# Conditioning products placed in four 32-column groups of the array, their parts summed by the product that transposes them

## The chip, the core and the metric

The kernel runs on one core of one Trainium2 chip. The metric is device time in microseconds (us); of several runs the median is taken. The core has a tensor engine (PE, with its weight loads shown apart as PEld), a vector engine (DVE), a scalar engine (ACT), GpSimd (POOL), and SyncE (SP), whose queue issues all the DMAs of this kernel.

## The reference, cut to what matters

The program computes a two-layer backbone over 1024 latent and 256 context tokens with 1024 channels. Each layer is steered by a conditioning vector; the change lies in how these conditioning values are computed, all in float32:

```
sc, scc = silu(c), silu(c_ctx)                                # 1024 each
for i in range(2):
    shift, scale, gate = split(sc @ ada_w[i] + ada_b[i], 3)         # ada_w[i]: 1024 x 3072
    shift_c, scale_c, gate_c = split(scc @ ada_w[i] + ada_b[i], 3)
    n_l = rmsnorm(h, norm_w[i]) * (1 + scale) + shift
    n_c = rmsnorm(hc, norm_w[i]) * (1 + scale_c) + shift_c
    y_l, y_c = layer_i(n_l, n_c)
    h, hc = h + gate * y_l, hc + gate_c * y_c
```

Layer 0 is retention and RWKV-7 side by side, layer 1 a Hyena convolution and neighbourhood attention.

## The kernel before, in words

The work comes in phases. `phase_a` (0 to some 690 us) norms the tokens, turns them channel-major and modulates them (`mod_tile`), projects them, and runs retention. `phase_b` (some 690 to 1290 us) runs RWKV in ten groups of 128 tokens, each with two recurrence steps (`recur`) and an inverse by 31 substitutions on DVE (lines 950 and 952). The later phases (output projection, second layer) follow.

The two conditioning vectors are kept as two columns, `self.sc`, [128, 8, 2]: channel k x 128 + p is in row p of slice k. `ada_block` (line 315) loads a block of n columns of `ada_w` as [128, 8, n] into a tile `aw`, and multiplies: eight products, the two columns of slice k stationary, the n columns of the weights moving, all added up in rows 0 and 1 of one PSUM tile `adaps` (line 321). A float32 product is shown in the trace as two matmul records with a weight load each, called passes here: 16 passes per block.

What is done with the two rows of sums differs:

- `ada_quarter` (layer 0, n = 256, eight blocks in the first 58 us): DVE copies the rows to SBUF (`adarow`, line 304), PE transposes each 128 columns by a product with a 2 x 2 identity (`adat`, line 307), DVE adds the bias. `mod_tile` needs the result.
- `ada_cols` (layer 1's shift and scale, n = 128, 16 blocks): the same with lines 284, 287 and 289.
- `ada_gate` (the gates of both layers, n = 128, 16 blocks): DVE adds the bias rows `adab` (two small DMAs, line 334, into a tile with one buffer) to the sums (line 335), and a DMA writes them to DRAM (line 336). Nothing is transposed.

In `phase_b` the 32 blocks of 128 columns are side work: first the gate of layer 0 (8 blocks), then `ada_cols` (16), then the gate of layer 1 (8). They share a PSUM pool with one buffer (`b_hp`, tag `mm`) with `RwkvOut`, which finishes RWKV's blocks. RWKV has a higher priority, and the planner that lays out each engine's instructions by simulated times fills the side work into the gaps. On the chip every engine then takes its instructions in that fixed order: an instruction that waits holds back all behind it on its engine.

Products that write only a part of PSUM's 128 rows use only the columns of the array that belong to these rows. `recur` has such products, 64 columns wide: at line 990 and 996 their outputs alternate between rows 0 to 63 and 64 to 127, at line 1002 eight go to one half, then eight to the other.

Of the kernel before, what the change touches and what calls it, by code (L numbers as in the profile page):

```python
# [10 lines left out]
F32 = mybir.dt.float32  # L11
# [3 lines left out]
ALU = mybir.AluOpType  # L15
AX = mybir.AxisListType
# [20 lines left out]
# ---------------------------------------------------------------- host layout  # L37
# [51 lines left out]
def dft_constants():  # L89
    """Two-stage DFT of 2048 real points, n = 8 n1 + n2, k = k1 + 256 k2, k1 = 0..127 with k1 = 128 in the place of the  # L90
    imaginary part of k1 = 0."""
# [69 lines left out]
def na_bias_layout(rpb):  # L161
    """[8, 15, 31] -> [8 heads, 2 row blocks, 3 column classes, 128 queries, 384 keys], with a fill outside the window."""
# [47 lines left out]
# ---------------------------------------------------------------- the kernel  # L210


class K:
# [23 lines left out]
    def ln_exp(self, out, x, scale, bias=None):  # L237
        """out = (scale x + bias) ** -0.5."""
        nc = self.nc
        if bias is None:  # L240
            nc.scalar.activation(out, x, AF.Ln, scale=scale)
        else:
            nc.scalar.activation(out, x, AF.Ln, scale=scale, bias=bias)
        nc.scalar.activation(out, out, AF.Exp, scale=-0.5)

    def rsqrt(self, pool, x, tag, n=1):
        """x: [P, n] positive -> its reciprocal square root; x is overwritten."""
# [16 lines left out]
    # ---- conditioning: 2 x 3072 modulation values per layer  # L264
    def ada_prepare(self, pool):
# [6 lines left out]
        self.sc = sc  # L272

    def ada_cols(self, layer, n, pool, psp, wbufs):
        """The column tile [P, (shift 8 | scale' 8), 2] of a layer's modulation, n columns at a time; a generator."""
# [5 lines left out]
        for blk in range(2048 // n):  # L281
            ps = self.ada_block(layer, blk * n, n, pool, psp, wbufs)
            rows = pool.tile([2, n], F32, name="adarow", tag="adarow", bufs=2)
            nc.vector.tensor_copy(rows, ps)
            pt = psp.tile([P, m, 2], F32, name="adat", tag="mm")
            for j in range(m):
                nc.tensor.matmul(pt[:, j, :], rows[:, j * P:(j + 1) * P], self.ident[0:2, 0:2], start=True, stop=True)
# [8 lines left out]
    def ada_quarter(self, layer, q, pool, psp, wbufs):  # L296
        """[P, (shift 2 | scale' 2), 2] of channel tiles 2 q, 2 q + 1."""
# [3 lines left out]
        for j in range(2):  # L301
            ps = self.ada_block(layer, j * DM + q * 256, 256, pool, psp, wbufs)
            rows = pool.tile([2, 256], F32, name="adarow", tag="adarow", bufs=2)
            nc.vector.tensor_copy(rows, ps)
            pt = psp.tile([P, 2, 2], F32, name="adat", tag="mm")
            for k in range(2):
                nc.tensor.matmul(pt[:, k, :], rows[:, k * P:(k + 1) * P], self.ident[0:2, 0:2], start=True, stop=True)
# [7 lines left out]
    def ada_block(self, layer, c0, n, pool, psp, wbufs):  # L315
# [4 lines left out]
        for k in range(8):  # L320
            nc.tensor.matmul(ps[0:2, :n], self.sc[:, k, :], w[:, k, :], start=k == 0, stop=k == 7)  # L321
        return ps[0:2, :n]

    def ada_gate(self, layer, n, pool, psp, wbufs):
        """A DRAM tile with the gate rows [2, 1024]; a generator."""
        nc = self.nc
        gd = self.gate[layer] = self.dram(f"gate{layer}", [2, DM])
        for c0 in range(0, DM, n):
            ps = self.ada_block(layer, 2048 + c0, n, pool, psp, wbufs)
            rows = pool.tile([2, n], F32, name="adarow", tag="adarow", bufs=2)  # L330
# [4 lines left out]
            nc.vector.tensor_tensor(rows, ps, ab, op=ALU.add)  # L335
            nc.sync.dma_start(gd[:, c0:c0 + n], rows)
            yield

    def norm_tile(self, xt, pool, tag):
        """xt [P, DM] token-major -> xt * rstd, in a tile of its own."""  # L340
# [9 lines left out]
    def modT(self, xns, t0, nhi, nlo, mc, v, pool, psp):  # L350
        """Normed token tiles xns (up to 4) -> columns t0.. of the transposed, modulated activations, split."""
# [3 lines left out]
    def mod_tile(self, xns, t0, nhi, nlo, k, sc, sh, pool, psp):  # L355
        """Channel tile k of it."""
# [11 lines left out]
    def wsplit(self, src, c0s, n, pool, tag="w", bufs=2, lo_eng=None, praw=None):  # L368
        """n columns of src [(8 P), .], in equal parts from each of c0s -> hi, lo float32r tiles [P, 8, n]."""
# [13 lines left out]
    def wtiles(self, src, c0s, pool, bufs, n=512):  # L383
        """512 columns of src, in equal parts from each of c0s -> hi(k), lo(k): float32r [P, 512], each in a tile of its
        own."""
# [15 lines left out]
    def mm3(self, ps, lh, ll, rh, rl, nk=8, start=True, stop=True):  # L401
        """ps += l.T @ r in three float32r passes; lh(k) etc. give operands."""
# [3 lines left out]
    def mm3_parts(self, ps, lh, ll, rh, rl, nk=8, start=True, stop=True):  # L406
        """mm3, as a generator that stops after every k."""
# [9 lines left out]
# ---------------------------------------------------------------- layer 0: projections and retention  # L417


def phase_a(s, D):  # L420
    """Activations, their projections, and retention. D: dict of DRAM tiles for what later phases read."""
# [56 lines left out]
class Shift:  # L478
    """RWKV's channels, channel-major, mixed with their neighbours in time."""
# [35 lines left out]
    def tokens(self, S, p):  # L515
        """S token-major, and with the tokens of each block of 128 in reverse."""
# [14 lines left out]
    def normed(self, S, p):  # L531
        """S of the k channels over the norm of its head's."""
# [13 lines left out]
    def run(self):  # L546
# [18 lines left out]
        # decay and rate activations  # L565
# [8 lines left out]
class Dense:  # L574
    """Retention's q, k, v (token-major, rotated) and the two gates, 512 columns of the projection at a time."""
# [18 lines left out]
    def qk(self, g):  # L594
        """Pairs 2g, 2g + 1: [pair][token][(q q k k v v), 64]."""
# [37 lines left out]
    def gate(self, nm, c0, turned):  # L633
        """2 silu(z), channel-major if turned."""
# [26 lines left out]
class Retention:  # L661
# [26 lines left out]
    def pair(self, p):  # L688
        """Heads 2p, 2p+1."""
# [89 lines left out]
# ---------------------------------------------------------------- layer 0: RWKV-7  # L779


def nat_block(d, g):
    """The 128-token block that direction d handles in group g: the context's two first, then the latent tokens'."""
# [3 lines left out]
def eye_lanes():  # L787
    """Row s = 2 i + l of the identity of 32, for lanes l * 64 + u: [P, 16, 32]."""
# [7 lines left out]
class Rwkv:  # L796
    """RWKV-7 in chunks of 64 tokens; groups of 2 chunk steps x 8 heads x 2 directions = 32 units. A unit index within a
    direction is (head parity h, step t, head pair p)."""
# [3 lines left out]
    def __init__(self, s, D, pg, pl, pc, pi, pf, pb):  # L802
# [14 lines left out]
        # operands that fill the tensor engine's rows, with zeros in the other head's, direction's or block's place  # L817
# [1105 lines left out]
```

## Time and profile before

| | |
|---|---|
| median of 3 runs | 2481.54 us (2480.74 to 2485.9) |
| span of the profiled execution | 2478.6 us |
| PE busy | 2301.3 us (93%), 16928 matmul passes |
| DVE busy | 1195.7 us (48%) |
| ACT, POOL busy | 931.3 us (38%), 786.5 us (32%) |
| passes of the conditioning products | 640, busy 111.8 us |
| mean granted TensorE clock | 0.941 |

The span goes from the first to the last instruction of one profiled execution; the median of the runs is 2.9 us longer. Busy time counts a pass from its start to its modelled end, so passes that overlap are counted once, and a busy PE is not PE at its peak. The granted clock is the share of full speed that the tensor engine had in a stretch.

### The profile page before, as it was taken

What the parts mean: (1) busy time and instruction counts of PE and PEld (TensorE: products, weight loads), DVE (VectorE), ACT (ScalarE), POOL (GpSimd) and SP (SyncE); (2) the same over time, 40 slices, a digit from 0 to 9 for tenths busy, and PEclk for the clock granted to TensorE, in tenths of its full rate; (3) what the DMA queues carried; (4) which work ended last, traced back from release to release, by engine and by line L of the source; (5) the groups of instructions that cost most, each with busy time, mean ns of one, the idle gap of its engine ahead of it and who ended that gap; (6) DMA issues with size and microseconds to landing.
All of it is one profiled execution on the core that took longest, in us unless ns stands there. A gap on an engine that the chain in (4) does not pass through costs nothing. (4 is left out here: it accounts for less than half of the span.)

```text
span 2478.6 us, 44427 instructions
## 1 busy us (share of the span) xinstructions
PE 2301.3 (93%) x16928; PEld 1879.3 (76%) x16928; DVE 1195.7 (48%) x3043; ACT 931.3 (38%) x1996; POOL 786.5 (32%) x1036
## 2 busy tenths in 40 slices
PE   7999999999988888888798999999899999989997
PEld 3778878777756777777686889889767777778987
DVE  6301212233348787677876546410145555534438
ACT  4321133545364444344254433321134333334432
POOL 2313617443656333333134433421101000010133
PEclk9999999999998677788898999999999999999999
DMA  7323334534386335565354334342465252265463
GB/s 241 94 72 111 109 113 139 162 113 127 107 227 177 84 99 135 135 146 142 82 169 147 125 120 137 121 150 76 118 176 149 84 143 71 63 202 150 127 187 124
DMA packets 398302, 325.68 MB, mean 131 GB/s; under 512 B 134974, under 2 KB 337864, under 8 KB 397834
## 3 DMA queue, kind: packets, MB, share of 16 engines
q1 hardware_dynamic: 398090, 322.85, 45.1%
q8 instruction: 134, 2.20, 0.4%
q14 instruction: 78, 0.64, 0.1%
HBM read 227.58 MB, written 95.17 MB: 130 GB/s over the span
## 5 line engine op out<-in xcount | busy, mean ns | idle before, releaser
L380 POOL TENSOR_TENSOR wlo<-wraw,whi 128x512 fp32r<-128x512 f32 (+1 forms) x60 | 81.7, 1379 | 414.6 <-ACT whi L379 351.7
L412 PE MATMUL dps<-n1hi,whi 128*128 128x512 f32 x448 | 195.1, 436 | 0.0
L412 PE MATMUL dps<-n1hi,wlo 128*128 128x512 f32 x448 | 177.0, 395 | 0.0
L412 PE MATMUL dps<-n1lo,whi 128*128 128x512 f32 x448 | 176.7, 394 | 0.0
L412 PE MATMUL dnp<-wlo,nhi 128*128 128x512 f32 x400 | 159.5, 400 | 2.9 <-POOL wlo L396 2.9
L412 PE MATMUL dnp<-whi,nlo 128*128 128x512 f32 x400 | 158.5, 398 | 0.0
L412 PE MATMUL dnp<-whi,nhi 128*128 128x512 f32 x400 | 154.7, 402 | 1.3 <-ACT whi L395 1.3
L396 POOL TENSOR_TENSOR wlo<-wraw,whi 128x512 fp32r<-128x512 f32 (+1 forms) x72 | 92.1, 1288 | 133.4 <-ACT whi L395 133.1
L412 PE MATMUL mmps<-nhi,whi 128*128 128x512 f32 (+1 forms) x336 | 123.4, 368 | 3.3 <-ACT vto L527 2.1
L321 PE MATMUL adaps<-aw,sc 128*2 128x128 f32 (+1 forms) x640 | 111.8, 330 | 11.7 <-DMA aw<-in_ada_w 10.0
L412 PE MATMUL mmps<-nlo,whi 128*128 128x512 f32 (+1 forms) x336 | 120.7, 361 | 0.0
L412 PE MATMUL mmps<-nhi,wlo 128*128 128x512 f32 (+1 forms) x336 | 119.4, 364 | 0.0
L950 DVE TENSOR_TENSOR tm<-RR,AL 128x126 f32<-128x126 f32 (+22 forms) x310 | 101.0, 326 | 18.8 <-DMA AL<-la 12.6
L412 PEld LDWEIGHTS dps<-n1hi,whi 128*128 128x128 f32 x448 | 84.8, 189 | 32.5 <-issue 21.7
L1248 POOL TENSOR_TENSOR hn<-hn,xr 128x256 f32<-128x256 f32 x60 | 47.2, 791 | 171.3 <-DVE hn L1247 159.3
L952 DVE TENSOR_TENSOR RR<-RR,tm 128x126 f32<-128x126 f32 (+22 forms) x310 | 96.8, 312 | 6.2
L412 PEld LDWEIGHTS dps<-n1hi,wlo 128*128 128x128 f32 x448 | 84.8, 189 | 18.8
L321 PEld LDWEIGHTS adaps<-aw,sc 128*2 128x2 f32 x640 | 54.7, 93 | 55.1 <-issue 15.2
L412 PE MATMUL ops<-whi,clo 128*128 128x256 f32 x320 | 90.6, 291 | 5.4 <-DVE clo L1181 5.4
L412 PEld LDWEIGHTS dps<-n1lo,whi 128*128 128x128 f32 x448 | 85.3, 190 | 10.5
L412 PEld LDWEIGHTS dnp<-wlo,nhi 128*128 128x128 f32 x400 | 76.0, 190 | 22.3 <-POOL wlo L396 4.6
L412 PE MATMUL ops<-wlo,chi 128*128 128x256 f32 x320 | 91.7, 288 | 0.0
(399 smaller groups left out, 6245.3 us busy)
## 6 DMA issues: line engine op xcount, KB each, us to landing
aw<-in_ada_w SPq DMA_DIRECT2D x32, 512.0 KB
kkr<-kkr SPq DMA_DIRECT2D x40, 384.0 KB
wraw<-in_odd_w_in SPq DMA_DIRECT2D x56, 256.0 KB
wraw<-in_even_w_in SPq DMA_DIRECT2D x48, 256.0 KB
bi<-in_nab SPq DMA_DIRECT2D x64, 192.0 KB
aw<-in_ada_w SPq DMA_DIRECT2D x8, 1024.0 KB
spec<-KS SPq DMA_DIRECT2D x32, 256.0 KB
h<-hn SPq DMA_DIRECT2D x16, 512.0 KB
```

Of the source, the lines that this page charges most:

```text
L321: nc.tensor.matmul(ps[0:2, :n], self.sc[:, k, :], w[:, k, :], start=k == 0, stop=k == 7)
L380: (lo_eng or nc.gpsimd).tensor_tensor(lo[:, kk:kk + 4], raw, hi[:, kk:kk + 4].bitcast(F32), op=ALU.subtract)
L396: nc.gpsimd.tensor_tensor(lo[:, :n], raw[:, :n], hi[:, :n].bitcast(F32), op=ALU.subtract)
L412: nc.tensor.matmul(ps, a, b, start=start and n == 0, stop=stop and n == 3 * nk - 1)
L950: nc.vector.tensor_tensor(t3, RR[:, 0:n, q:q + 1].to_broadcast([P, n, w]), AL[:, q:q + 1, q + 1:32].to_broadcast([P, n, w]), op=ALU.mult)
L952: nc.vector.tensor_tensor(RR[:, 0:n, q + 1:32], RR[:, 0:n, q + 1:32], t3, op=ALU.add)
L1248: add.tensor_tensor(h[:, cs], h[:, cs], x[:, cs], op=ALU.add)
```

## The change

Only the conditioning is changed, and the descriptor space of GpSimd's own DMAs. The stationary operand becomes 32 columns wide (two with values, 30 with zeros). Product k writes rows 32 (k mod 4) to 32 (k mod 4) + 31 of PSUM, so each of the four row groups holds the sum of two of the eight slices. The whole [128, n] PSUM tile is copied to SBUF, and the transposing product uses, in the place of the 2 x 2 identity, a matrix `sel` [128, 2] that has ones at the rows 32 g + j of column j: it adds the four parts as it transposes. For the gates, which were not transposed, a product with `sel` as the stationary operand is new (`adag`); its sums get the bias in the `adab` tile, from which they are written out.

```
 def ada_prepare
-        self.sc = sc
+        self.sc = self.cp.tile([P, 8, 32], F32, name="scw")
+        nc.gpsimd.memset(self.sc, 0.0)
+        nc.vector.tensor_copy(self.sc[:, :, 0:2], sc)
+        self.sel = self.cp.tile([P, 2], F32, name="sel")
+        nc.vector.tensor_reduce(self.sel, self.ident.rearrange("p (g c) -> p c g", g=4)[:, 0:2, :], axis=AX.X, op=ALU.add)
 def ada_cols (and ada_quarter, with 256 for n)
-            rows = pool.tile([2, n], F32, name="adarow", tag="adarow", bufs=2)
+            rows = pool.tile([P, n], F32, name="adarow", tag="adarow", bufs=2)
             nc.vector.tensor_copy(rows, ps)
...
-                nc.tensor.matmul(pt[:, j, :], rows[:, j * P:(j + 1) * P], self.ident[0:2, 0:2], start=True, stop=True)
+                nc.tensor.matmul(pt[:, j, :], rows[:, j * P:(j + 1) * P], self.sel, start=True, stop=True)
 def ada_block
         for k in range(8):
-            nc.tensor.matmul(ps[0:2, :n], self.sc[:, k, :], w[:, k, :], start=k == 0, stop=k == 7)
-        return ps[0:2, :n]
+            g = 32 * (k % 4)
+            nc.tensor.matmul(ps[g:g + 32, :n], self.sc[:, k, :], w[:, k, :], start=k < 4, stop=k > 3)
+        return ps[:, :n]
 def ada_gate
-            rows = pool.tile([2, n], F32, name="adarow", tag="adarow", bufs=2)
+            rows = pool.tile([P, n], F32, name="adarow", tag="adarow", bufs=2)
...
-            nc.vector.tensor_tensor(rows, ps, ab, op=ALU.add)
-            nc.sync.dma_start(gd[:, c0:c0 + n], rows)
+            nc.vector.tensor_copy(rows, ps)
+            ps = psp.tile([P, 512], F32, name="adag", tag="mm")
+            nc.tensor.matmul(ps[0:2, :n], self.sel, rows, start=True, stop=True)
+            nc.vector.tensor_tensor(ab, ps[0:2, :n], ab, op=ALU.add)
+            nc.sync.dma_start(gd[:, c0:c0 + n], ab)
 def kernel
-    nc = bacc.Bacc("TRN2", target_bir_lowering=False, num_devices=1)
+    nc = bacc.Bacc("TRN2", target_bir_lowering=False, num_devices=1, dynamic_dma_scratch_size=4096)
```

The new columns take 1 KB more of each SBUF partition; the last line gives GpSimd's own DMA descriptors less of it.

## Rows read from the trace of the kernel before

**Rows 1.** The stretches of the program: busy us of each engine with its instructions, the granted clock (PEclk), the DMA engines' busy share and GB/s. Columns: from:to, length, PE, PEld, DVE, ACT, POOL, PEclk, DMA, GB/s.

```profile
62.00:640.00 578.00, 560.38 (x2812) 439.83 (x2811) 146.60 (x288) 204.98 (x366) 241.57 (x344) 0.99 0.39 115
690.00:747.00 57.00, 51.86 (x399) 36.80 (x398) 33.77 (x78) 38.02 (x98) 34.64 (x53) 0.97 0.81 219
747.00:800.00 53.00, 47.83 (x311) 35.58 (x312) 45.35 (x121) 23.22 (x64) 33.31 (x56) 0.81 0.68 178
800.00:927.00 127.00, 106.11 (x1519) 95.94 (x1517) 98.75 (x271) 56.21 (x135) 43.01 (x71) 0.73 0.38 94
927.00:1193.00 266.00, 230.03 (x3236) 196.14 (x3236) 199.40 (x573) 108.31 (x248) 93.06 (x155) 0.83 0.53 132
```

**Rows 2.** The same stretches for line 321 alone, the conditioning products (PE and PEld busy, then clock, DMA, GB/s); below them the groups of the same line by shape (busy us, mean ns of one | idle time of the engine before them).

```profile
690.00:747.00 57.00, 18.18 (x127) 9.77 (x125) 0.97 0.81 219
747.00:800.00 53.00, 17.94 (x96) 9.22 (x96) 0.81 0.68 178
927.00:1193.00 266.00, 43.58 (x288) 24.78 (x288) 0.83 0.53 132
...
L321 PE MATMUL adaps<-aw,sc 128*2 128x128 f32 x512 | 80.1, 312 | 2.3 <-DVE mc L289 1.1 <-DVE adarow L335 0.7 <-DMA aw<-in_ada_w 0.6
...
L321 PE MATMUL adaps<-aw,sc 128*2 128x256 f32 x128 | 31.7, 405 | 9.4 <-DMA aw<-in_ada_w 9.4
```

**Rows 3.** PE in order of time, products that use one half of the array's columns: start, us until the last one's end, engine, line, shape, count.

```profile
1042.66 0.22 PE L1010 MATMUL rp<-UV,Gr 128*64 128x64 f32 x1
1042.66 0.22 PE L1002 MATMUL sp<-UV,BT 128*64 128x64 f32 x1
...
1042.78 0.92 PE L1010 MATMUL rp<-UV,Gr 128*64 128x64 f32 x15
...
1195.30 1.15 PE L990 MATMUL rp<-UV,Ga 128*64 128x64 f32 x32
```

**Rows 4.** The first 60 us: two stretches (columns as in rows 1), then PE in order of time.

```profile
35.00:40.00 5.00, 3.15 (x17) 1.42 (x16) 4.81 (x14) 1.96 (x4) 1.25 (x2) 1.00 1.09 348
40.00:60.00 20.00, 19.16 (x112) 10.99 (x109) 15.73 (x29) 7.64 (x13) 9.35 (x8) 1.00 0.14 42
...
7.78 5.01 PE L321 MATMUL adaps<-aw,sc 128*2 128x256 f32 x16 [7.78 <-DMA aw<-in_ada_w]
...
39.67 3.62 PE L321 MATMUL adaps<-aw,sc 128*2 128x256 f32 x16
...
50.96 3.62 PE L321 MATMUL adaps<-aw,sc 128*2 128x256 f32 x16
...
58.48 1.18 PE L412 MATMUL dnp<-whi,nhi 128*128 128x512 f32 x4
```

**Rows 5.** Around one block of the gates: PE in order of time.

```profile
694.26 1.69 PE L321 MATMUL adaps<-aw,sc 128*2 128x128 f32 x14
695.88 0.71 PE L851 MATMUL lora<-wa,w 64*128 64x128 f32 x4
696.52 0.38 PE L321 MATMUL adaps<-aw,sc 128*2 128x128 f32 x2
696.83 0.49 PE L746 MATMUL rsp<-qT 64*128 64x128 f32 x4
```

**Rows 6.** Small operations beside the products: the rows of sums on DVE (count: shortest/median/longest ns), the transposing product and another product with two moving columns but 128 rows (busy us, mean ns).

```profile
L335 DVE TENSOR_TENSOR adarow<-adaps,adab x16: 269/272/279, 693.2 to 1193.3; 2x128 f32<-2x128 f32 x16
L284 DVE COPY adarow<-adaps x16: 271/272/279, 751.8 to 1094.8; 2x128 f32<-2x128 f32 x16
...
L747 DVE TENSOR_TENSOR sT<-rsp,Dm 128x128 f32<-128x128 f32 x12 | 2.8, 275 | 2.0 <-PE rsp L746 2.0
...
L287 PE MATMUL adat<-cst,adarow 2*128 2x2 f32 x32 | 7.1, 288 | 11.5 <-DVE adarow L284 11.4
L1069 PE MATMUL bon<-rkh,fp 128*128 128x2 f32 x40 | 6.8, 292 | 2.3 <-POOL fp L1064 2.3
```

**Rows 7.** Waits between 690 and 1250 us (who for whom: us in total, times, longest), and one block's last products on PE with its rows of sums on DVE, in order of time.

```profile
PE adat L287 <- DVE adarow L284: 11.4, 4, 4.7
...
1155.82 1.91 PE L321 MATMUL adaps<-aw,sc 128*2 128x128 f32 x16
...
1165.89 0.28 DVE L335 TENSOR_TENSOR adarow<-adaps,adab 2x128 f32<-2x128 f32 x1
```

**Rows 8.** RWKV's recurrence: line 987 alone in two stretches (16 passes open each step; PE and PEld busy, clock, DMA, GB/s), and a place where PE and DVE meet, in order of time.

```profile
822.80:927.10 104.30, 8.47 (x64) 7.52 (x64) 0.74 0.42 103
927.10:1193.20 266.10, 20.42 (x160) 18.61 (x160) 0.83 0.53 133
...
1036.52 3.15 PE L321 MATMUL adaps<-aw,sc 128*2 128x128 f32 x14
1039.59 1.44 PE L1010 MATMUL rp<-UV,Gr 128*64 128x64 f32 x11
...
1042.98 0.69 DVE L1004 TENSOR_TENSOR S<-S,sp 128x512 f32<-128x512 f32 x1 [3.51 <-PE sp L1002]
```

**Rows 9.** SP's queue around the write of a gate block, in order of time, and the DMA queue that carried the data (packets, MB, share).

```profile
696.50 0.49 SPq L336 DMA_DIRECT2D gate<-adarow  x1
697.04 0.54 SPq L334 DMA_DIRECT2D adab<-in_ada_b  x2
...
q1 hardware_dynamic: 398090, 322.85, 45.1%
```

More of the change, by code (lines that the diff above doesn't have):

```diff
@@ L302, in ada_quarter @@
             ps = self.ada_block(layer, j * DM + q * 256, 256, pool, psp, wbufs)
-            rows = pool.tile([2, 256], F32, name="adarow", tag="adarow", bufs=2)
+            rows = pool.tile([P, 256], F32, name="adarow", tag="adarow", bufs=2)
             nc.vector.tensor_copy(rows, ps)
@@ L306, in ada_quarter @@
             for k in range(2):
-                nc.tensor.matmul(pt[:, k, :], rows[:, k * P:(k + 1) * P], self.ident[0:2, 0:2], start=True, stop=True)
+                nc.tensor.matmul(pt[:, k, :], rows[:, k * P:(k + 1) * P], self.sel, start=True, stop=True)
             b = o + 8 * j + 2 * q
```

## The prediction

> **What bounds the kernel now.** I read four views, in this order: the busy time by stretches, the conditioning products' own part of each stretch, PE in order of time where they stand, and who waits for whom.
>
> The stretches show where PE time is worth anything. From 62 to 640 us PE is busy for 560 of 578 us: whatever ends sooner before it makes the program shorter by as much [rows 1]. From 690 to 747 PE is busy 51.9 of 57 us and the other compute engines at most 38: PE sets the pace. From 747 to 800 PE (47.8 of 53) and DVE (45.4) are both nearly full. From 927 to 1193 it is 230 and 199 of 266, and the recurrence runs from engine to engine.
>
> The conditioning products take part in each: 127 passes from 690 to 747, 96 up to 800, none from 800 to 927, 288 up to 1193 [rows 2], and 128 passes of 256 columns before 58 us. Two of their passes from 696.52 let the next product start at 696.83, so 0.31 us; fourteen from 694.26 take 1.62. The twelve more cost 1.31 us: 0.109 us a pass, and 0.09 us once per run of them [rows 5]. A block of 16 passes is then 1.74 us of PE, and 3.5 with 256 columns (3.62 to the end of the last [rows 4]).
>
> **What the new layout does to a block.** Whether products in different column groups run side by side is seen in the recurrence: at 1042.66 two products for different halves start together. Where the halves alternate, 32 passes take 1.15 us to the end of the last, where one half is used alone, 15 take 0.92 [rows 3]. With 0.22 us for the last pass, that is 30 ns a pass against 50. But the two passes of one product use the same columns and follow each other. If PE starts its passes in order, the second pass of product k runs beside the first of product k + 1, and nothing else can: two groups are busy at a time, though four are there. Eight products then need 9 times 0.109 us and not 16 times: 0.76 us less for 128 columns, 1.52 for 256. The same ratio as in rows 3 (0.6) would make it 0.70. I take 0.76; the bounds are none and, with all four at once, some 5 pass times a block: 1.2 us less.
>
> Here the Trainium skill is bolder: "TensorE: Matmul & The Clock Gate", in its part on packing small matmuls by row and column tiling, lets tiles start some 4 ns apart and reports three column tiles at 2.38 times the speed. By it the block would come near a quarter. Rows 3 have only two halves and can't tell that from pairs. It is the first rival below.
>
> **Part A, the first 60 us.** Up to 40 us transfers run at 348 GB/s or more with their engines full; PE's first product waits 7.78 us for weights; a faster block there ends at the same transfer. From 40 to 60 us the DMA is at 0.14, PE busy 19.2 of 20, DVE 15.7. Three blocks run in it, the first from 39.67, the last from 50.96 [rows 4]: 3 x 1.52 = 4.6 us less. DVE allows 20 - 15.7 = 4.3. The projections start at 58.48, partly behind their own weights. I take 3.5 us; bounds 0 and 4.3. The new `scw` and `sel` are made before 7.78 us.
>
> **Part B, 690 to 747.** Eight gate blocks save 8 x 0.76 = 6.1 us of the engine that sets the pace. Each also gets the adding product: two passes in a run of their own, 0.31 us [rows 5], so 2.5 us. And this product waits for a copy on DVE, with PE's queue behind it. The nearest row is the transposing product, which does just that: four waits, 11.4 us in 16 blocks, 0.71 a block [rows 7]. DVE is 59% busy here against 75% and more later, so I take half, 8 x 0.36 = 2.8 us; bounds 0 and 5.7. Net 0.8 us less; from 3.6 less to 2.1 more.
>
> **Part C, 747 to 800.** Six blocks of layer 1's columns at a clock of 0.81 save 6 x 0.76 / 0.81 = 5.6 us of PE. DVE is as full, so I count half, 2.8 us; bounds 0 and 5.6.
>
> **Part D, 927 to 1193.** Eighteen blocks at 0.83 save 16.5 us of PE. How much of it was on the path? Four recurrence steps without any conditioning take 104.3 us, 26.1 each; ten with 18 blocks take 266.1, 26.6 each [rows 8]. So 43.6 us of PE [rows 2] cost some 5 us of path, one eighth. One eighth of 16.5 is 2.0. Against that stands one place where the path is seen: 14 passes from 1036.52 hold back lines 1010 and 1002, and DVE then idles 3.51 us for them [rows 8]; and the stretch without blocks had the lower clock, 0.74 against 0.83. So I take 3.0, and give back 1.0 for eight adding products, their waits and copies (8 x (0.31 + 0.71 + 0.27) = 10.3 us on engines, one eighth rounded down). Net 2.0; bounds 3 more, 8 less (half of 16.5).
>
> **Edits at nothing.** Copying [128, n] in the place of [2, n]: 275 ns for 128 x 128 from PSUM, 272 for 2 x 128 [rows 6]. The transposing product with 128 rows: 292 ns beside 288. Eight more copies in B are 2.2 us of a DVE with 23 us free. The bias tile is now read by a DMA, and the next block's bias must wait for that: on SP the load follows the write by 0.5 us [rows 9], so the queue may stand still for a transfer's time, 16 times, with RWKV's loads behind it. I cost it at nothing, since the planner can put other issues between the two; three times that 0.5 us in all 16 blocks, at D's one eighth, would be 3 us, within D's bound. All data moves on the hardware queue, so GpSimd's smaller descriptor space changes nothing.
>
> **Sum.** 3.5 + 0.8 + 2.8 + 2.0 = 9.1 us less than the profiled span of 2478.6: 2469.5. The runs' median is 2.9 us above the span: 2472.4 us. The likeliest case alone spans 2466 to 2477.
>
> **Rivals.**
> - Four groups at once. A is held by DVE at 4.3; B becomes 8 x 1.2 - 5.3 = 4.3, C 6 x 1.2 / 0.81 / 2 = 4.4, D one eighth of 26, so 3: 16 us, 2465.5. For it: four groups are there. Against: passes in order. 0.13.
> - Hidden: only part A comes through, since the recurrence and DVE set phase B. Rows 8 speak for it in D, rows 1 against it in B. 2478. 0.22.
> - The adding product holds PE back; this one is slower. It stands in PE's queue where the planner thinks its copy is done; the copy can lag, as from 1157.73 (end of the products) to 1165.89 [rows 7], and all of RWKV behind it waits. Without waits the change saves 3.5 + 3.6 + 2.8 + 2.7 = 12.6. If all 16 wait 2.85 us, the mean of the four waits in rows 7, the first eight cost 22.8 in full and the later an eighth, 2.8: 13 us slower, 2494; with two thirds of them 2486. It decides from 1.2 us a block in the first eight ((12.6 - 2.8) / 8). Against: 0.71 in rows 7. 0.16.
> - No overlap at all, so the change doesn't do what it says: every block as before, plus the adding products, 2.5 + 2.8 in B and 1 in D: 2487.5. Rows 3 speak against it. 0.07.
>
> **How the numbers follow.** My forecast gets 0.42. The planner lays out phase B anew, and 16 more products shift everything behind them; this widens every case by some us. A measurement of this kernel tells about 0.2% (5 us) from no change. Faster than 2476.5: most of the forecast and the first rival, 0.54. Within 5 us: hidden and the edges of its neighbours, 0.24. Slower than 2486.5: the third rival, the fourth, and a share of bad layouts, 0.22. The range is 2460 (all bounds good but a part of D) to 2488 (the third rival at two thirds).
>
> **What would show it.** In the changed profile: starts of line 321's products in pairs some 0.1 us apart, a block near 1 us (0.5 for four at once, 1.7 for none); the first projection near 55 us; PE busy from 690 to 747 below 52 us; PE's waits before the adding product, in total and each; the recurrence's steps from 927 on near 26 us. The prediction is wrong if the blocks get shorter and the steps don't, or if the waits for the copied rows exceed 10 us before 750.

## The result, and the profile after

The changed kernel takes 2493.7 us (median of 5 runs, 2490.8 to 2500.1); the kernel before, on the same chip, 2480.9 us. The ratio is 1.0057, with a 95% interval from 1.0034 to 1.0079: slower by 0.6%. I had forecast 2472.4 us and a range up to 2488; the measured time lies above it.

The stretches of the profiled execution after, with the columns of [rows 1] (from:to, length, PE, PEld, DVE, ACT, POOL, PEclk, DMA, GB/s):

```profile
62.00:640.00 578.00, 561.96 (x2848) 442.85 (x2847) 148.94 (x291) 204.13 (x368) 247.05 (x356) 0.99 0.39 116
690.00:747.00 57.00, 50.74 (x350) 36.72 (x350) 31.86 (x77) 36.68 (x94) 38.05 (x59) 0.65 0.63 171
747.00:800.00 53.00, 44.55 (x344) 36.77 (x344) 46.78 (x126) 20.14 (x54) 25.76 (x45) 0.56 0.64 162
800.00:927.00 127.00, 106.50 (x1556) 95.53 (x1550) 100.83 (x283) 59.74 (x144) 48.32 (x78) 0.80 0.45 118
927.00:1193.00 266.00, 218.99 (x3258) 191.68 (x3258) 204.20 (x575) 108.88 (x247) 91.96 (x154) 0.79 0.52 130
```

From 690 to 800 us the granted clock is 0.65 and 0.56, where it was 0.97 and 0.81 [rows 1]. Between the two levels, 2.4 and 1.2 GHz, these means are 70% and 88% of the stretches at the lower one. The conditioning products alone, in the same stretches (PE, PEld and DVE busy, then clock, DMA, GB/s; [rows 2] has them before):

```profile
690.00:747.00 57.00, 6.41 (x96) 3.39 (x96) 1.72 (x6) 0.65 0.63 171
747.00:800.00 53.00, 5.58 (x64) 2.68 (x64) 0.83 (x3) 0.56 0.64 162
...
927.00:1193.00 266.00, 16.81 (x278) 8.63 (x278) 5.12 (x18) 0.79 0.52 130
```

In the first of them they take 11.8 us less than before (6.41 against 18.18, with 96 passes for 127), and yet PE as a whole is busy only 1.1 us less (50.74 against 51.86). PE in order of time, in the first stage and at a block of the gates, shows how fast a block has become:

```profile
7.34 1.93 PE L327 MATMUL adaps<-aw,scw 128*32 128x256 f32 x16 [7.34 <-DMA aw<-in_ada_w]
...
47.61 1.07 PE L327 MATMUL adaps<-aw,scw 128*32 128x256 f32 x16
...
52.43 1.18 PE L421 MATMUL dnp<-whi,nhi 128*128 128x512 f32 x4
...
684.78 1.08 PE L327 MATMUL adaps<-aw,scw 128*32 128x128 f32 x16
...
688.00 0.59 PE L343 MATMUL adag<-adarow,sel 128*2 128x128 f32 x2
```

Sixteen passes of 256 columns take 1.07 us where they took 3.62 [rows 4]. Their records start four at a time, the rounds 216 to 240 ns apart. At the lower clock, as at 7.34 us, the rounds are 427 ns apart and the block takes 1.93 us. The 5.01 us of the first block before are no match for that: its passes start 378 to 427 ns apart at first and some 216 later, so the clock rose within it. The block of 128 columns at 684.78 also stands at the lower clock; at full clock such a block takes 0.64 to 0.65 us. The first projection starts at 52.43 us and not at 58.48. So the part that does the work is better than I thought, and the loss has to be found elsewhere.

I followed it by landmarks, the first or last product of a kind in the trace, after against before: first projection -6.0 us; last transpose `gtp` (192 us) -10.6; last `mmps` product (676 us) -10.0; first `up` product of the recurrence (813 us) -0.4; last step's start (1280 us) -0.9; first projection of layer 1 (1565 us) +14.9; end +13.3. So a lead of 10 us is lost before 813 us, and 15.8 us more between 1280 and 1580, where there is no conditioning product at all. What stands there are the Hyena filters (`hkps`, `d1ps` and what follows them) and the output projection `ops`.

Of the lead of 10 us, 4.6 came between 58 and 192 us, where the products are the same as before. There the granted clock is 0.987 after and 0.962 before; over 134 us the difference is an estimated 3.4 us. The runs below agree: 0.987 to 1.000 with four groups in layer 0, 0.949 to 0.975 without.

### The profile page after: what moved, and what is told of

It reads as the page before. It is cut to its first block, busy times and chain, and to the rows that moved or that the text cites. A ratio compares the mean times of both kernels' runs of the same rounds, so it can differ in the third digit from the quotient of the medians.

```text
span 2491.9 us, 44552 instructions
## 1 busy us (share of the span) xinstructions
PE 2286.5 (92%) x16960; PEld 1887.2 (76%) x16960; DVE 1201.6 (48%) x3061; ACT 931.7 (37%) x1996; POOL 786.4 (32%) x1037
## 5 line engine op out<-in xcount | busy, mean ns | idle before, releaser
L924 PE MATMUL sc<-AR,BK 64*128 64x128 f32 x640 | 98.2, 332 | 6.0 <-DVE Gr L928 4.1
L421 PEld LDWEIGHTS dps<-n1hi,wlo 128*128 128x128 f32 x448 | 84.4, 188 | 18.5
L924 PEld LDWEIGHTS sc<-AR,BK 64*128 64x128 f32 x640 | 86.9, 232 | 12.5 <-issue 8.3
L421 PE MATMUL ops<-whi,chi 128*128 128x256 f32 x320 | 95.1, 299 | 0.0
L421 PEld LDWEIGHTS dps<-n1lo,whi 128*128 128x128 f32 x448 | 84.8, 189 | 10.4
```

The costliest lines, as they stand in the source:

```text
L421: nc.tensor.matmul(ps, a, b, start=start and n == 0, stop=stop and n == 3 * nk - 1)
L924: nc.tensor.matmul(ps[:, p, :], bks[d, p // 2][HALF[h], u, :], R["ar"][d, p // 2][HALF[h], u, :], start=True, stop=True)
```

## The experiments

Three theories. **Clock**: with shorter conditioning products PE is idler around 690 to 820 us, the granted clock falls, and the other products pay. **Adding product**: `adag`, its copy and its waits hold the queue. **Order**: the tile planner lays out the whole program anew, and it is that order that costs the time; the change's own work is not the reason. In what follows a ratio is to the kernel before on the same chip, with its 95% interval.

**One nudge, and the parts apart.** The kernel before with the smaller descriptor space alone (`e1_scratch`), and the changed kernel with the products of a block in another order (`e2_grouporder`):

```diff
-    nc = bacc.Bacc("TRN2", target_bir_lowering=False, num_devices=1)
+    nc = bacc.Bacc("TRN2", target_bir_lowering=False, num_devices=1, dynamic_dma_scratch_size=4096)
```

```diff
-        for k in range(8):
+        for k in (0, 4, 1, 5, 2, 6, 3, 7):
             g = 32 * (k % 4)
```

The changed kernel with the old block and the old rows, here `ada_block2`, in `ada_cols` and `ada_gate` (`e3_layer0`), or in `ada_quarter` (`e4_phaseb`):

```diff
-            ps = self.ada_block(layer, blk * n, n, pool, psp, wbufs)
-            rows = pool.tile([P, n], F32, name="adarow", tag="adarow", bufs=2)
+            ps = self.ada_block2(layer, blk * n, n, pool, psp, wbufs)
+            rows = pool.tile([2, n], F32, name="adarow", tag="adarow", bufs=2)
```

> The kernel before with nothing but GpSimd's smaller descriptor space, which moves the tiles in memory and lets the planner change a few places after 1300 us. Clock theory (the shorter conditioning products leave PE idler from 640 to 820 and from 1190 to 1300 us, its granted clock falls, and the rest of PE's work there takes longer) and adding-product theory (the extra product and its copy hold the queue): nothing changes, within 4 us of before. Order theory (the planner's other order behind 1280 us costs the 14 us, and any nudge gives another order): within 4 us if the few places don't matter, off by 5 to 12 us either way if small nudges do.

Measured: 2488.3 us, 1.001 (0.9989 to 1.003). It can't be told from no change, which fits all three.

> The changed kernel with the eight products of a block in the order of the column groups (0, 4, 1, 5, 2, 6, 3, 7), so that the four passes of one group stand one behind the other: about 13 of 16 pass times instead of 4 to 5, the same instructions otherwise. All theories: a 256-column block takes about 3 us at full clock, and most of the 10.6 us that were gained before 130 us are lost again (gain left 1 to 3 us). Clock theory: the granted clock from 690 to 800 us comes back to 0.85 or more and the program lands near before plus the adding products, 2478 to 2486 us. Adding-product theory: the loss in phase B stays and the early gain is gone, 2497 to 2506 us. Order theory: the order is planned anew once more, so the time is not tied to the clock: anywhere from 2475 to 2510, with the step from 1280 to 1580 us deciding.

Measured: 2472.3 us, 0.9958 (0.9936 to 0.998), faster than before and below every range given, the order theory's by 3 us. My expectation that a block would take about 3 us fell. The same block as above, PE in order of time:

```profile
47.80 1.09 PE L327 MATMUL adaps<-aw,scw 128*32 128x256 f32 x16
```

In the program the two products of a group now stand one behind the other, and still sixteen passes take 1.09 us: their records start in rounds of four, 216 to 240 ns apart, as in the changed kernel. That the order did change shows within a round: the starts are 13 ns apart here and 7 in the changed kernel. So this run is the changed kernel with equal work and equal block times, at a clock as low (0.68 and 0.62 in the two stretches). The clock theory had expected 0.85. Neither clock nor adding product can explain that the ratio is 1% lower than the changed kernel's; the order can.

> Four groups in layer 0 alone (the first 60 us); the blocks beside the recurrence in their two-row form, without the adding product. Clock theory and adding-product theory: the 10.6 us gained by 130 us are kept to the end, and the clock from 690 to 800 us stays at 0.9 or more: 2468 to 2473 us. Order theory: the same gain, but the planner lays phase B out anew, so 2460 to 2485, and the step from 1280 to 1580 us tells which.

Measured: 1.0012 (0.9994 to 1.003). The clock from 690 to 747 us is 0.94 and there is no adding product, but nothing is gained over the kernel before. The two theories that name them expected 2468 to 2473 us; it was 2486.1, 1 us above the order theory's range. In its trace the lead is -10.4 us at 192 us, -7.7 at 676 and -2.1 at 813.

> Four groups beside the recurrence alone, with the adding product; layer 0 in its two-row form. Clock theory and adding-product theory: the early gain is absent and the loss stays, 2500 to 2506 us, with a granted clock of 0.6 to 0.7 from 690 to 800 us. Order theory: the loss was of the changed kernel's order alone, 2475 to 2500 us.

Measured: 2517.9 us, 1.0132 (1.0101 to 1.0164). All three missed, the two rivals by 12 us and the order theory by 18. In its trace the recurrence's last step ends 33.7 us late. Of this, 7.1 us are there at 676 us, ahead of its four-group blocks, and 17.9 at 813. What costs the rest is not shown; as this is one order, a cost of the changed blocks beside the recurrence stays possible here.

**The order alone.** The count that follows is taken from the program as the planner laid it out: how many products of the Hyena filters stand on PE ahead of the recurrence's last step (each is two passes in the trace), and how many ahead of the first output projection. The order of the products in a block can move these counts, since the planner simulates the program as it places it. `v1_pairs` and `v2_reversed` differ from the changed kernel in the tuple of the loop above alone. `e5_gates_old` takes the old `ada_gate` and block back for the gates, and `h2_filters_first` adds to the changed kernel

```diff
-        for _ in hy:
-            pass
+        with tc.high_priority(offset=1000000):
+            for _ in hy:
+                pass
```

and the like, with 500000, for each step of the filters inside phase B.

> The changed kernel with the products of a block in the order 1, 0, 3, 2, 5, 4, 7, 6; every product, copy and group is the same. Only the planner's order of the program moves: before the recurrence's last step stand 18 Hyena filter products hkps and 16 transforms d1ps (the changed kernel 14 and 8, the group order 24 and 20; before the change 24 and 16), and 96 hkps before the first output projection (86, 112, 108). Order theory: the time follows these counts and lies between the changed kernel and the group order, 2478 to 2489 us. Clock theory and adding-product theory: nothing that they name is changed against the changed kernel, 2490 to 2497 us.

> The changed kernel with the products of a block in the order 3, 2, 1, 0, 7, 6, 5, 4; the same work. Its order has 24 hkps and 20 d1ps before the recurrence's last step and 112 hkps before the first output projection, as the group order has. Order theory: 2467 to 2477 us. Clock theory and adding-product theory: as the changed kernel, 2490 to 2497 us.

> Four groups in layer 0 and in the columns of layer 1, the gates in their two-row form without the adding product. Its order has 16 hkps and 12 d1ps before the recurrence's last step and 90 hkps before the first output projection, nearly as in the changed kernel. Adding-product theory: the extra product, its copy and its waits are gone, so the loss is gone, 2470 to 2480 us. Order theory: as bad as the changed kernel, 2486 to 2496 us. Clock theory: half of the shortened blocks in phase B are back, so about half of the loss, 2478 to 2488 us.

> The changed kernel with a higher priority for the Hyena filters in the planner, beside the recurrence's last two steps and behind them; the same work. Its order has 18 hkps and 16 d1ps before the recurrence's last step and 112 hkps before the first output projection (the changed kernel 14, 8 and 86). Order theory: part of the 14 us between 1280 and 1580 us comes back, 2478 to 2487 us. Clock theory and adding-product theory: as the changed kernel, 2490 to 2497 us.

Measured: `v1_pairs` 2479.1 us, 0.9972 (0.9957 to 0.9987); `v2_reversed` 2475.7 us, 0.9972 (0.9953 to 0.9991); `e5_gates_old` 2489.0 us, 1.0013 (0.9997 to 1.003); `h2_filters_first` 2485.7 us, 1.000 (0.9981 to 1.0019). All four lie inside what the order theory gave, and none where the adding-product theory had it. The clock theory's range for `e5_gates_old` ended 1 us lower.

**The change without its second part, and the kernel before, in other orders.** `t1_layer0_bad` and `t2_layer0_good` are `e3_layer0` with another tuple in the loop of its four-group block. `h3_best` joins the group order with the priority of `hy` behind phase B. `b2_before_nudged` is the kernel before with this:

```diff
+            ab = pool.tile([2, n], F32, name="adab", tag="adabr", bufs=1)
+            src = self.i["ada_b"][layer:layer + 1, 2048 + c0:2048 + c0 + n]
+            for j in range(2):
+                nc.sync.dma_start(ab[j:j + 1, :], src)
             ps = self.ada_block(layer, 2048 + c0, n, pool, psp, wbufs)
             rows = pool.tile([2, n], F32, name="adarow", tag="adarow", bufs=2)
-            ab = pool.tile([2, n], F32, name="adab", tag="adabr", bufs=1)
...
```

> Four groups in layer 0 alone, as in the run e3_layer0, with the products of a block in the order 3, 2, 1, 0, 7, 6, 5, 4. Every block beside the recurrence keeps its two-row form, so neither the clock theory nor the adding-product theory has anything to act on. The planner's order has 14 hkps and 8 d1ps before the recurrence's last step and 86 hkps before the first output projection, the counts of the changed kernel. Order theory: the 10 us gained by 130 us are lost behind 1280 us as in the changed kernel, 2486 to 2498 us, at a granted clock near 0.9 from 690 to 747 us. Both others: 2468 to 2476 us.

> The same with the order 1, 0, 3, 2, 5, 4, 7, 6: 24 hkps and 16 d1ps before the last step, 96 hkps before the first output projection. Order theory: 2471 to 2482 us, at least 8 us below the run with 14 and 8. Both others: no difference between the two.

> The kernel before with the gates' bias loads ahead of the products that they belong to, nothing of the change in it. Its order has 16 hkps and 12 d1ps before the recurrence's last step and 104 hkps before the first output projection (before: 24, 16 and 108). Order theory: 3 to 10 us slower than before. Clock theory and adding-product theory: within 3 us of before.

> The group order (0, 4, 1, 5, 2, 6, 3, 7) of the changed kernel, and the Hyena filters that are left behind phase B at a higher priority: 24 hkps and 20 d1ps before the last step, 116 hkps before the first output projection. Order theory: as the group order or a little better, 2466 to 2474 us.

Measured: `t1_layer0_bad` 2493.6 us, 1.005 (1.0029 to 1.0072), as the order theory had it. `t2_layer0_good` 2492.4 us, 1.0043 (1.0022 to 1.0064): a miss, by 10 us and more. `b2_before_nudged` 2500.0 us, 1.0072 (1.0044 to 1.010): moving the two small loads of each gate block costs 18 us, more than the whole change does and more than I had allowed. In its trace SP's queue is not seen waiting at the moved loads. The time goes in the recurrence: ten steps take 284.6 us, 18.5 more than before. `h3_best` 2477.8 us, 0.9984 (0.9963 to 1.0005): a miss by 4 us, no better than the group order alone.

The miss of `t2_layer0_good` shows that the counts hold only a part of the order. Its stretch behind the recurrence is good, 7.7 us shorter than before; but its recurrence ends 17.4 us late, and that is no matter of Hyena filters.

**Does the order inside a block matter by itself, and does the clock follow the blocks?** `v3_same_order` and `v4_group_order_again` change the loop's order so that everything else in the program stays where it is. `e6_refill_two` and `e6_refill_four` run the products of the blocks in phase B two and four times (the diff is of the first; the second has a 4):

```diff
-        for k in range(8):
+        for k in (0, 4, 1, 5, 2, 6, 3, 7) * (1 if n == 256 else 2):
```

> The changed kernel with the products of a block in the order 0, 2, 1, 3, 4, 6, 5, 7. The planner's order of all other instructions on all five engines is the changed kernel's, to the last one. Order theory: the changed kernel's time, 2489 to 2498 us. If the order of a block's own products were what made the group order fast: 2470 to 2480 us.

> The changed kernel with the products of a block in the order 0, 4, 2, 6, 1, 5, 3, 7. The planner's order of all other instructions is that of the group order (0, 4, 1, 5, 2, 6, 3, 7), to the last one. Order theory: the group order's time, 2467 to 2477 us, and 12 us or more below the run with the changed kernel's order.

> The group order, and beside the recurrence each block's products run twice over (the second time into the same place from the start, so that the result is the same): 32 passes a block where the changed kernel has 16. Clock theory: the granted clock from 690 to 800 us rises above the 0.68 and 0.62 of the group order. If the clock there does not hang on how long PE works at the blocks: 0.6 to 0.7. Its order has 16 hkps and 8 d1ps before the last step and 112 hkps before the first output projection, so the order theory expects a slower tail than the group order whatever the clock.

> The same with four times the products, 64 passes a block, about the PE time of the two-row form. Clock theory: the granted clock from 690 to 800 us comes back to 0.8 or more, as in the kernel before (0.97, 0.81). If it does not hang on that: 0.6 to 0.7. Its order has no hkps before the recurrence's last step, so its own time is above 2500 us by the order theory.

Measured: `v3_same_order` 2498.2 us, 1.0059 (1.0036 to 1.0082): the changed kernel's 1.0057 again, 0.2 us above the range given. `v4_group_order_again` 2473.0 us, 0.996 (0.9941 to 0.9978), the group order's 0.9958 again. This is the cleanest pair: the same work on the same chip, two orders of the program, 25 us apart; and each order gives its time twice, whatever the order inside the block. The traces bear the equal orders out. Of the 16320 PE passes that are not conditioning products, all but 16 start in the same sequence in `v3_same_order` as in the changed kernel, and all in `v4_group_order_again` as in the group order; so do all entries of SP's queue in both pairs. Between the changed kernel and the group order 13477 of the 16320 stand in the same place.

`e6_refill_two` took 2471.2 us, 0.9948 (0.9922 to 0.9975), `e6_refill_four` 2512.2 us, 1.0114 (1.007 to 1.0158, from two runs). The stretches from 690 and from 747 us, columns as above, first of the group order and then of the run with twice the products:

```profile
690.00:747.00 57.00, 53.00 (x359) 38.36 (x359) 33.33 (x81) 39.02 (x99) 40.07 (x62) 0.68 0.69 186
747.00:800.00 53.00, 44.64 (x385) 37.99 (x385) 45.67 (x129) 20.09 (x53) 24.97 (x44) 0.62 0.63 162
```

```profile
690.00:747.00 57.00, 50.50 (x428) 36.08 (x429) 30.94 (x74) 34.94 (x89) 34.38 (x53) 0.85 0.68 175
747.00:800.00 53.00, 42.46 (x341) 34.55 (x334) 41.07 (x106) 18.19 (x51) 29.03 (x50) 0.59 0.57 150
```

With twice the products the clock of the first stretch comes back to 0.85 (0.88 with four times), that of the second does not (0.59 both times). So the fall from 690 to 747 us does hang on how much the conditioning products keep PE at work; the one from 747 to 800 was not brought back by this. `e5_gates_old` fits: with the gates in the old form and the columns in the new, the clock is 0.85 in the first stretch, where the gates stand, and 0.60 in the second, where the columns stand. With both in the old form (`e3_layer0`, `t1_layer0_bad`, `t2_layer0_good`) it is 0.87 to 0.94 and 0.78 to 0.82. My expectation of a slow tail for `e6_refill_two` was a miss: its recurrence ended 11.6 us early and the stretch behind was as long as before.

All runs by their profiled executions. "Filters" is the number of `hkps` passes ahead of the end of the recurrence's last `rp<-SP` product; the next two columns are the time of that end, and of layer 1's first projection, after minus before; the last is their difference. One execution is one draw: those of one kernel spread over some 20 us, so the ratio, from 2 to 12 runs, is the verdict, and the columns only tell where time went.

| kernel | ratio | filters | last step, us | layer 1, us | between, us |
|---|---|---|---|---|---|
| before | 1 | 48 | 0 | 0 | 0 |
| after | 1.0057 | 28 | -0.9 | +14.9 | +15.8 |
| v3_same_order | 1.0059 | 28 | +0.7 | +19.9 | +19.2 |
| e2_grouporder | 0.9958 | 48 | -2.0 | -5.3 | -3.3 |
| v4_group_order_again | 0.996 | 48 | +5.7 | -0.6 | -6.3 |
| v2_reversed | 0.9972 | 48 | +0.3 | -6.1 | -6.4 |
| v1_pairs | 0.9972 | 36 | -4.3 | -1.9 | +2.4 |
| h3_best | 0.9984 | 48 | +0.6 | -5.7 | -6.3 |
| h2_filters_first | 1.0 | 36 | +12.3 | +9.8 | -2.5 |
| e5_gates_old | 1.0013 | 32 | +8.7 | +17.2 | +8.5 |
| e3_layer0 | 1.0012 | 36 | +2.4 | +2.2 | -0.2 |
| t1_layer0_bad | 1.005 | 28 | -4.7 | +7.8 | +12.5 |
| t2_layer0_good | 1.0043 | 48 | +17.4 | +9.7 | -7.7 |
| e1_scratch | 1.001 | 48 | +6.9 | +6.0 | -0.9 |
| b2_before_nudged | 1.0072 | 32 | +20.5 | +20.6 | +0.1 |
| e4_phaseb | 1.0132 | 48 | +33.7 | +37.3 | +3.6 |
| e6_refill_two | 0.9948 | 32 | -11.6 | -12.2 | -0.6 |
| e6_refill_four | 1.0114 | 0 | -28.6 | +28.3 | +56.9 |

The stretch between follows the filters at the ends: with 28 passes ahead it is 12 to 19 us longer, with none 57 us, with 48 between 8 shorter and 4 longer. From 32 to 36 it goes either way. What moves the last step by up to 34 us these counts do not tell.

Where the 15.8 us are can be read from the groups of instructions on PE (line, operation, shape, count | busy us, mean ns of one | idle time before them), from 1150 to 1280 and from 1280 to 1600 us. The kernel before:

```profile
L1320 PE MATMUL hkps<-hw,hid 64*128 64x128 f32 x48 | 9.4, 425 | 0.5 <-DMA hw<-in_hw 0.5
L1333 PE MATMUL d1ps<-f,EO 128*128 128x128 f32 x32 | 5.4, 319 | 0.2 <-ACT S L1362 0.2
...
L1320 PE MATMUL hkps<-hw,hid 64*128 64x128 f32 x210 | 52.2, 431 | 5.9 <-DVE HK L1321 2.5 <-ACT KS L1341 1.8 <-ACT S L1362 1.5
L1333 PE MATMUL d1ps<-f,EO 128*128 128x128 f32 x224 | 33.9, 297 | 1.7 <-ACT KS L1341 1.1 <-POOL EO L1326 0.2 <-ACT S L1362 0.2
```

The changed kernel:

```profile
L1329 PE MATMUL hkps<-hw,hid 64*128 64x128 f32 x28 | 7.3, 459 | 1.0 <-DMA hw<-in_hw 1.0
L1342 PE MATMUL d1ps<-f,EO 128*128 128x128 f32 x16 | 3.2, 364 | 0.0
...
L1329 PE MATMUL hkps<-hw,hid 64*128 64x128 f32 x228 | 57.7, 428 | 3.7 <-ACT KS L1350 3.2 <-ACT d2r L1384 0.2 <-ACT S L1371 0.2
L1342 PE MATMUL d1ps<-f,EO 128*128 128x128 f32 x240 | 35.8, 293 | 1.8 <-POOL EO L1334 0.9 <-ACT KS L1350 0.3 <-POOL EO L1335 0.2
```

The group order:

```profile
L1329 PE MATMUL hkps<-hw,hid 64*128 64x128 f32 x48 | 9.3, 447 | 3.6 <-DMA hw<-in_hw 3.6
L1342 PE MATMUL d1ps<-f,EO 128*128 128x128 f32 x40 | 7.6, 349 | 0.2 <-ACT S L1371 0.2
...
L1329 PE MATMUL hkps<-hw,hid 64*128 64x128 f32 x208 | 49.7, 430 | 1.9 <-ACT d2r L1384 1.9
L1342 PE MATMUL d1ps<-f,EO 128*128 128x128 f32 x216 | 34.5, 308 | 2.7 <-DVE HK L1330 2.2 <-POOL EO L1335 0.5
```

The group order does 48 and 40 passes beside the recurrence's last steps, the kernel before 48 and 32. The changed kernel does 28 and 16, and the rest stands behind 1280 us, where PE is the bound: busy 283.2 of the 300.7 us from the start of the last step to layer 1's first projection, against 270.1 of 284.8 before and 267.1 of 281.5 in the group order. These two groups alone are 7.4 us longer behind 1280 than before (57.7 + 35.8 against 52.2 + 33.9). The other part is the output projection, which the changed kernel starts 22 us early, at 1382.6, between the filters that are left: its 960 passes cover 140.3 us of PE there, 130.0 before and 129.3 in the group order. Some of this is the clock. The passes stand 0.21 us apart at 1383 us in the changed kernel, and 0.12 at 1405 in the group order:

```profile
1383.07 0.41 PE L421 MATMUL ops<-whi,clo 128*128 128x256 f32 x1
1383.29 0.41 PE L421 MATMUL ops<-whi,chi 128*128 128x256 f32 x1
...
1405.26 0.28 PE L421 MATMUL ops<-whi,chi 128*128 128x256 f32 x1
1405.38 0.28 PE L421 MATMUL ops<-wlo,chi 128*128 128x256 f32 x1
```

In the changed kernel 51 of the passes start at the lower clock and cover 12.7 us; at the group order's 0.135 us each (129.3 / 960), where none does, they would cover an estimated 6.9. So some 6 of the 11 us between these two are the lower clock. Where the other 5 come from is not shown.

## Why the prediction was wrong

The step that the forecast failed on is the planner's new order, which the prediction took for "some us" of spread and gave no term in the sum; it is worth 25 us, and the last paragraphs of this part have it. Of the 22.4 us between the forecast of 9.1 less and the measured span (13.3 more), 8.2 are missing at the end of the last step (0.9 less) and 15.8 come behind it, where the sum has nothing; the stretch from layer 1 on gives 1.6 back. The parts in turn:

**Part A** was right in kind and too small. The step of it that failed, which made the forecast too slow and not too fast, is "If PE starts its passes in order, the second pass of product k runs beside the first of product k + 1, and nothing else can". The passes start four at a time, in both orders of the products above, so a block is 2.5 us shorter and not 1.52. The bound "DVE allows 20 - 15.7 = 4.3" fell too: the first projection starts 6.0 us earlier, and 10.6 us are gained by 192 us, where I took 3.5; the clock behind 58 us, which the sum left out, is a part of that. The first rival had the mechanism right, at 0.13. The Trainium skill's page "TensorE: Matmul & The Clock Gate" (Part 3: Packing small matmuls) is borne out in its speedup: it has 2.38 times for three column tiles, and here four give 3.62 / 1.07 = 3.4 times. The same section says that matmuls start and end in program order and are never reordered; by that the group order's block should have been far slower than the changed kernel's, and it took 1.09 us against 1.07, so the measurement decides.

**Part B and C**: I had 0.8 and 2.8 us less; the lead went from 10.0 us at 676 to 0.4 at 813 instead of growing. The waits that I feared were not the reason: in the changed kernel PE waits for the copied rows before an adding product twice in 16 blocks, 2.2 us in all, and the same wait before the transposing product fell from 11.4 us [rows 7] to 2.4. The rows of PE's waits from 640 to 1200 us, and the view of who waited for the adding product and its result:

```profile
PE adat L292 <- DVE adarow L289: 2.4, 3, 1.4
PE adag L343 <- DVE adarow L341: 2.2, 2, 1.7
...
who waited for it (us, times):
  PEld adaps L327: 6.2, 3
  PE adaps L327: 5.7, 2
  DVE adab L344: 2.2, 3
  PEld ryp L761: 0.3, 1
```

The wait that I did not name is the larger one: twice the next block's products wait, 5.7 us in all, for the bank that the adding product's sum is read from. The third rival gave 2494 us with waits for the copied rows in all 16 blocks, and 2493.7 were measured; that its number came so near is luck, as its waits are not there. Of my two signs of being wrong, waits over 10 us before 750 us did not show, and whether the steps got shorter can't be told (part D); both looked at the edits alone. What I left out altogether is the clock. PE's busy time in B hardly fell because the passes around the blocks became longer: [rows 1] against the first fence here, 0.97 against 0.65. A group of the recurrence's own products in that stretch, before and after:

```profile
L851 PE MATMUL lora<-wa,w 64*128 64x128 f32 x32 | 5.7, 297 | 0.4 <-ACT tw L855 0.3
```

```profile
L860 PE MATMUL lora<-wa,w 64*128 64x128 f32 x32 | 8.7, 418 | 3.9 <-ACT tw L864 3.9
```

But the clock does not account for the lost lead: `e3_layer0` and `t1_layer0_bad` have the old blocks and 0.94 and 0.92 there, and they too come from -7.7 and -8.1 us at 676 to -2.1 at 813. With a clock of 0.65 to 0.68 the lead shrinks by 5.2 to 9.6 us in the eight runs with the changed work, with 0.85 to 0.94 by 5.6 to 9.5 in four others (those two, `t2_layer0_good` and `e5_gates_old`). Why a lead of 6 to 12 us shrinks so there is open; only `v2_reversed` (6.1 us at 813) and `e6_refill_four` (7.3) kept more than half of it.

**Part D** came near in this one execution, and that shows nothing. Ten steps take from 921.85 to 1185.10, 263.3 us, against 266.1 before [rows 8]: 2.8 us less, where I had 2.0. But `v3_same_order`, with the same order of the program, takes 267.6 for the same steps, the group order 266.9, and `v2_reversed` 257.3; a gain of 2 us can't be told from this spread.

```profile
921.85 2.36 PE L996 MATMUL rp<-SP,AR 128*128 128x128 f32 x16
...
1185.10 2.05 PE L996 MATMUL rp<-SP,AR 128*128 128x128 f32 x16 [0.98 <-ACT SP L1017]
```

**What the sum did not have.** "The planner lays out phase B anew, and 16 more products shift everything behind them; this widens every case by some us." This is the sentence that was mis-sized. The size is 25 us between two orders of one and the same work, and 18 us for moving small loads in the kernel before. The gain of 9 us that I had summed up from the edits is smaller than that. In the group order the kernel takes 2472.3 us, 0.1 us from my forecast, and that confirms nothing: in its own order it takes 2493.7, and the views that I read told nothing of either order. It was wrong to draw the range from bounds on the edits alone, and to stop the sum at 1193 us because no edit lies behind it. Two slips in the working change nothing there: a block of 16 passes at 0.109 us with 0.09 once is 1.83 us and not 1.74, where only differences were used, and the fourth rival's terms add up to 2487.8 and not 2487.5.

What the change brings by itself can only be told over several orders. Its four orders (the changed kernel's, the group order's, `v1_pairs`, `v2_reversed`) have a mean of (1.0057 + 0.9958 + 0.9972 + 0.9972) / 4 = 0.999, and `h2_filters_first` (1.0) and `h3_best` (0.9984) leave it there. Layer 0 alone, in three orders, has (1.0012 + 1.005 + 1.0043) / 3 = 1.0035; the part beside the recurrence alone was run in one order (1.0132). The kernel before is itself one order of its work, and `e1_scratch` (1.001) and `b2_before_nudged` (1.0072) are two more. So few orders do not tell any of these from no change, nor what became of the 10 us that layer 0 gains early.

A version that beats both kernels is the changed one in the group order: 0.9958 and, with the other order inside the block, 0.996, the intervals ending at 0.998 and 0.9978. Running the products of phase B twice gives 0.9948 (0.9922 to 0.9975), which is not told apart from it.

## What to carry to other kernels

Where a planner orders the program, an edit has two effects, its work and a new order of everything, and the second can be the larger: before a gain or a loss of less than 1% is put down to the edit, build the same work in two or three other orders and time them. Look for the loss also where no edit is, above all at work that fills the gaps of a chain: what no longer fits in front of the chain's end stands behind it, and the stretch there was 12 to 57 us longer where 28 passes or none stood in front. And where a filler on PE is made faster, look at the granted clock of its stretch after: where it fell here, from 0.97 to 0.65, the products beside it took 418 ns and not 297. What that cost in the kernel's time was not shown.

## What the runs showed that I had not expected

- Products for different column groups run side by side whatever their order in the program: 16 passes of 256 columns take 1.07 us in the changed kernel and 1.09 us with each group's products one behind the other. Only the starts within a round tell the orders apart, 7 or 13 ns.
- Doubling the products of the 32 blocks in phase B made the kernel no slower (0.9948 against 0.9958), in the order that the planner made for it; the clock from 690 to 747 us was 0.85 instead of 0.68.
- The order of the products in a block, which hardly changes the block's own time, could make the planner lay out the whole program anew; `v3_same_order` and `v4_group_order_again` left the rest of theirs as it was.
- Repeated runs of the kernel before spread over 23 us on one chip (2472.0 to 2495.3 in the last session), so three runs tell less than the 0.2% that I took as the limit.
